# One more feed-forward unit by plain products: block products begin with unit 6 instead of unit 5

## The chip, the cores and the metric

The kernel runs on one core of a Trainium2 chip. The metric is device time in microseconds (us) of one execution; the time of a kernel is the median of its runs. Five engines work side by side: TensorE (PE in the profile; its weight loads are PEld), VectorE (DVE), ScalarE (ACT), GpSimd (POOL) and SyncE (SP, which issues most of the transfers).

## The reference

Two layers of an encoder over 512 tokens of width 1024, in float32. Each layer adds an attention mixer, a cross-attention over 256 memory tokens and a feed-forward part to `x`; a last RMSNorm closes. The change touches the feed-forward part alone:

```python
def conv_ffn(h, w_up, conv_w, conv_b, w_down):
    u = h @ w_up                                  # 512 x 1024 @ 1024 x 5632
    up = jnp.pad(u, ((0, 0), (1, 1), (0, 0)))
    u = up[:, :-2] * conv_w[0] + up[:, 1:-1] * conv_w[1] + up[:, 2:] * conv_w[2] + conv_b
    gate, val = jnp.split(u, 2, axis=-1)          # 2816 columns each
    return (jax.nn.silu(gate) * val) @ w_down
...
x = x + conv_ffn(rms_norm(x, norm_ffn[l]), w_up[l], conv_w[l], conv_b[l], w_down[l])
```

## The kernel before

**Numbers.** TensorE multiplies a rounded format, so each float32 operand is kept as two parts, `hi` (the rounded value) and `lo` (what is left). A plain product is three matmuls (hi by hi, hi by lo, lo by hi) of 128 x 512, which `mm3` writes; all matmuls are recorded on line 101, a helper, so they are told apart by the tiles that they write and read.

**Units.** The 2816 gate and 2816 value columns are cut into 22 units of 128 columns of each. Activations lie with channels on the partitions and the 512 tokens along the free axis. The units run in order; of each unit come a gate and a value array, a width-3 convolution of both (`convolve`: on ACT line 1884 and, on DVE, four instructions of line 1891 for each array, two of them 504 columns wide and two 7), Silu on ACT, a product of both (DVE line 1894) and the split into hi and lo for the down projection (ACT line 1079, DVE line 1080).

**Plain units** (`j < PLAIN`): 8 chunks of 128 channels by three matmuls, for gate and for value: 48 matmuls of 128 x 512. They read the normalised input in `ffn.hi` and `ffn.lo` (tiles `xg`). DVE scales both arrays by the token norm (line 1871) before `convolve`.

**Block units** (`j >= PLAIN`): gate and value of a unit are got by seven half-sized products instead of eight, in the manner of Strassen and Winograd. The tokens are cut into two halves and the channels into two halves; `up_forms` multiplies seven weight forms by seven input forms. A product is 4 chunks of one matmul of 128 x 512 (weight hi by input hi and lo side by side) and one of 128 x 256 (weight lo by input hi), 56 matmuls for a unit. Three banks `a` (tag mm), `b` (tr) and `c` (sc) collect them, and DVE and POOL add pieces between products: three reductions (DVE line 1963) and five additions of 128 x 256 (DVE lines 1971, 1979, 1983, 1984, 1989) for each unit, with ACT copies and POOL additions (lines 1970, 1982) between.

**Forms.** The weight forms `sums` and `diffs` are made ahead in HBM by transfers (`make_form`, an accumulating transfer on POOL's queue), in shares of a few units (`SHARES_OF_FORMS`). The input forms are made once in each layer: `scale_tokens` (DVE line 1913) after unit 0, `token_sums` (DVE and POOL, lines 1924 to 1928) and the splits of `t2` and `t1` after unit 2, and the splits of `t3`, `b22` and `t4` after the last plain unit, because those three are written over `ffn.hi` and `ffn.lo`, which the plain products read until then. In a split, ACT writes hi (lines 1939, 1942) and DVE (POOL for `b22`) writes lo (lines 1940, 1943).

**Weights.** Each weight tile of 512 KB is loaded (SP), rounded to hi by ACT (line 789) and its lo is taken by POOL (line 790), of `sums` by DVE (line 790).

**Down rows.** The units lie in groups (0 to 5, 6 to 11, 12 to 16, 17 to 21). While a group's units run, the rows of the down projection of the group before run between their products (`sequence`); a row of group 0 is 6 plain products of 512 columns, one for each unit. Unit 6 has one row behind it, units 7 to 11 two or less each.

**Order.** The order on PE, ACT, DVE and POOL is set when the program is built: the class `Order` replays the program with costs, moves instructions to where it expects them to be ready, and tries several rounds. So an edit in one place can move instructions anywhere. PE may take later products ahead of ones that are not ready, within the turn of the banks.

Of the kernel before, what the change touches and what calls it, by code (L numbers as in the profile page):

```python
# [35 lines left out]
TURNED = 2  # L36


PLAIN = 5
SHARES_OF_FORMS = [(5, 4), (9, 4), (13, 4), (17, 5)]  # L40
HALF = S // 2
EPS = 1e-6
BIG = 3.0e38
# [640 lines left out]
def encoder_kernel(ctx: ExitStack, tc: tile.TileContext, t: dict, out: bass.AP):  # L684
# [16 lines left out]
    made = [[[dpool.tile([D, P * n], F32, name=f"dr_{what}{l}{j}") for what in ("sums", "diffs")]  # L701
             for j, n in SHARES_OF_FORMS] for l in range(DEPTH)]
    form_queue = [(l, g, n) for l in range(DEPTH) for g in range(len(SHARES_OF_FORMS)) for n in range(4)]

    def make_form(upto=DEPTH):
# [4 lines left out]
        l, g, n = form_queue.pop(0)  # L710
        j, nj = SHARES_OF_FORMS[g]
        w, half = t["w_up"][l], D // 2
# [108 lines left out]
    def plan_up(l, what, j):  # L821
        if what == "up":
            cols(("up", j, 0), t["w_up"][l], 0, KC, P * j, P)
            cols(("up", j, 1), t["w_up"][l], 0, KC, D_FF + P * j, P)
            return
        (g, j0), = [(g, j0) for g, (j0, n) in enumerate(SHARES_OF_FORMS) if j0 <= j < j0 + n]
        if what == "gate":
# [8 lines left out]
    def sequence():  # L836
# [4 lines left out]
        for g, (j0, nj) in enumerate(GROUPS):  # L841
            row = 0
            for j in range(j0, j0 + nj):
                to = 0 if g == 0 else min(KC, 2 * (j - j0) + 1) if j < j0 + nj - 1 else KC
                rows, row = range(row, to), to
                if j < PLAIN:
                    yield "up", j, None
# [350 lines left out]
    for l in range(DEPTH):  # L1198
# [675 lines left out]
        def convolve(j, us):  # L1874
            cs = []
            for side in range(2):
                ch = side * NF + j
                u = us[side]
                if side and j >= PLAIN:
                    w = [minus[:, l, i, j : j + 1] for i in range(3)]  # L1880
# [49 lines left out]
        def split_form(name, where=None):  # L1930


            place = xform[name] = [rtile((2, S)) for _ in range(2)] if where is None else [where[:, :2], where[:, 2:]]
            direct = {"b11": (0, 0), "b21": (1, 0), "b22": (1, 1)}
            for i, v in enumerate(place):
                hi, lo = (v[:, :, half] for half in halves)
                src = quarter(*direct[name])[i] if name in direct else raw_forms[name][:, 2 * i : 2 * i + 2]
                if name in ("t1", "t4"):
                    ACT.mul(hi, src, -1.0)
                    DVE.scalar_tensor_tensor(lo, src, -1.0, f(hi), op0=ALU.mult, op1=ALU.subtract)  # L1940
                else:
                    ACT.copy(hi, src)
                    (POOL if name == "b22" else DVE).tensor_sub(lo, src, f(hi))  # L1943
# [162 lines left out]
        for what, n, rows in sequence():  # L2106
# [15 lines left out]
            elif n > 1:  # L2122
                up(n)
                if n == 2:
                    token_sums()
                    split_form("t2")
                    split_form("t1")
                elif n == PLAIN - 1:
                    split_form("t3", ffn.hi[:, :4])
# [94 lines left out]
```

## Time and profile before

| | before |
|---|---|
| median of 3 runs (lowest to highest) | 1323.54 us (1323.25 to 1324.92) |
| the profiled execution, its own time | 1324.15 us |
| its span in the trace | 1322.3 us |
| mean granted TensorE clock | 0.995 |
| PE, DVE, POOL, ACT busy share of the span | 98%, 70%, 65%, 59% |

The page gives busy times over the whole span. TensorE's share is near one everywhere, but its matmuls are pipelined, so that a recorded one (0.39 us) is longer than the distance to the next one; what TensorE loses is better seen from starts, in a stretch whose number of matmuls is known. The timeline gives starts, the windows give the busy time of each engine and the granted clock in a stretch.

### The profile page before, as it was taken

What the parts mean: (1) busy time and instruction counts of PE and PEld (TensorE: products, weight loads), DVE (VectorE), ACT (ScalarE), POOL (GpSimd) and SP (SyncE); (2) the same over time, 40 slices, a digit from 0 to 9 for tenths busy, and PEclk for the clock granted to TensorE, in tenths of its full rate; (3) what the DMA queues carried; (4) which work ended last, traced back from release to release, by engine and by line L of the source; (5) the groups of instructions that cost most, each with busy time, mean ns of one, the idle gap of its engine ahead of it and who ended that gap; (6) DMA issues with size and microseconds to landing.
All of it is one profiled execution on the core that took longest, in us unless ns stands there. A gap on an engine that the chain in (4) does not pass through costs nothing.

```text
span 1322.3 us, 19671 instructions
## 1 busy us (share of the span) xinstructions
PE 1297.9 (98%) x6715; PEld 1098.2 (83%) x6715; DVE 924.8 (70%) x1883; ACT 781.7 (59%) x1473; POOL 861.2 (65%) x656
## 2 busy tenths in 40 slices
PE   9999999999989999999999999999998999999997
PEld 8888888888878888888888878888887788888887
DVE  6559876675995676666635697775769866666675
ACT  6677776665654554554645687765644545555554
POOL 3657966737666677767745678665566666766673
PEclk9999999999999999999999999999998999999999
DMA  9733698678599788796556427958882455554541
GB/s 285 223 110 102 188 238 195 200 169 221 147 230 241 221 232 219 199 256 171 170 144 191 144 64 210 261 136 257 188 190 77 130 150 151 159 148 141 154 144 64
DMA packets 290564, 235.46 MB, mean 178 GB/s; under 512 B 7712, under 2 KB 246816, under 8 KB 290464
## 3 DMA queue, kind: packets, MB, share of 16 engines
q1 hardware_dynamic: 273152, 198.16, 50.5%
q0 software_dynamic: 16896, 35.65, 15.1%
q8 instruction: 53, 0.87, 0.3%
q14 instruction: 47, 0.39, 0.1%
q10 hardware_dynamic: 416, 0.39, 0.1%
HBM read 224.22 MB, written 73.40 MB: 225 GB/s over the span
## 4 chain that ended last, share of the span: by engine, by line
PE 87%; DVE 9%; ACT 2%; issue 1%; DMA 1%; POOL 0%; POOLq 0%; ACTq 0%; DVEq 0%
PE mm L101 64%; PE sc L101 16%; PE tr L101 4%; PE tr L1586 2%; DVE t L1891 2%; DMA raw<-dr_sums 1%; PE tr L1431 1%; DVE r L1943 1%; DVE lo L790 1%; DVE t L1963 1%; PE tr L1780 1%; DVE r L1080 0%; ACT hi L789 0%; DVE sc L1403 0%; DVE r L1913 0%
## 5 line engine op out<-in xcount | busy, mean ns | idle before, releaser
L790 POOL TENSOR_TENSOR lo<-raw,hi 128x512 fp32r<-128x512 f32 (+3 forms) x327 | 567.3, 1750 | 279.0 <-ACT hi L789 237.0
L789 ACT CAST hi<-raw 128x1024 fp32r<-128x1024 f32 (+2 forms) x365 | 291.2, 813 | 287.5 <-issue 82.4
L101 PE MATMUL mm<-r,hi 128*128 128x512 f32 (+1 forms) x1360 | 442.3, 392 | 6.7 <-DVE t L1963 3.7
L101 PEld LDWEIGHTS mm<-r,hi 128*128 128x128 f32 x1360 | 249.0, 188 | 59.0 <-DVE t L1963 4.0
L101 PE MATMUL mm<-r,lo 128*128 128x512 f32 (+1 forms) x848 | 291.2, 346 | 0.0
L101 PE MATMUL mm<-xg,hi 128*128 128x512 f32 x784 | 258.8, 395 | 4.0 <-DVE sc L1984 2.8
L101 PEld LDWEIGHTS mm<-r,lo 128*128 128x128 f32 x848 | 160.1, 189 | 22.4
L101 PE MATMUL mm<-xg,lo 128*128 128x256 f32 (+1 forms) x528 | 176.6, 334 | 0.0
L101 PEld LDWEIGHTS mm<-xg,hi 128*128 128x128 f32 x784 | 145.8, 188 | 35.2 <-DVE sc L1984 2.3
L101 PE MATMUL mm<-hi,xg 128*128 128x512 f32 (+1 forms) x384 | 111.7, 360 | 0.0
L101 PEld LDWEIGHTS mm<-xg,lo 128*128 128x128 f32 x528 | 99.7, 189 | 11.9
L101 PE MATMUL sc<-xg,hi 128*128 128x512 f32 x328 | 109.0, 395 | 0.0
L1086 POOL TENSOR_SCALAR t<-t,s 128x512 f32<-128x512 f32 (+1 forms) x112 | 67.7, 627 | 43.5 <-DVE s L1570 20.1
L1982 POOL TENSOR_TENSOR t<-t 128x256 f32<-128x256 f32 x34 | 42.4, 1248 | 62.6 <-ACT t L1981 62.6
L1989 DVE TENSOR_TENSOR sc<-mm,t 128x256 f32<-128x256 f32 x34 | 14.7, 432 | 88.4 <-ACT t L1988 88.4
L101 PEld LDWEIGHTS mm<-hi,xg 128*128 128x128 f32 x384 | 68.0, 189 | 9.2 <-DVE r L1280 0.2
L101 PE MATMUL sc<-xg,lo 128*128 128x256 f32 (+1 forms) x232 | 75.4, 327 | 0.0
L101 PE MATMUL sc<-r,r 128*128 128x256 f32 (+1 forms) x352 | 73.2, 329 | 0.0
L101 PEld LDWEIGHTS sc<-xg,hi 128*128 128x128 f32 x328 | 61.4, 188 | 14.0 <-ACT xg L78 0.4
L101 PE MATMUL sc<-r,hi 128*128 128x512 f32 x200 | 72.6, 405 | 0.1
L101 PE MATMUL mm<-lo,xg 128*128 128x512 f32 (+1 forms) x192 | 68.4, 356 | 0.0
L1080 DVE TENSOR_TENSOR r<-tr,r 128x512 fp32r<-128x512 f32 x82 | 55.7, 685 | 14.2 <-ACT r L1079 10.1
(222 smaller groups left out, 2457.2 us busy)
## 6 DMA issues: line engine op xcount, KB each, us to landing
raw<-in_w_up SPq DMA_DIRECT2D x54, 512.0 KB, 4.7
raw<-dr_sums SPq DMA_DIRECT2D x34, 512.0 KB, 4.3
raw<-dr_diffs SPq DMA_DIRECT2D x34, 512.0 KB, 4.3
raw<-in_w_in SPq DMA_DIRECT2D x25, 512.0 KB, 5.0
dr_sums<-in_w_up SPq DMA_DIRECT2D x12, 1024.0 KB, 7.5
dr_diffs<-in_w_up SPq DMA_DIRECT2D x12, 1024.0 KB, 9.1
raw<-in_w_down SPq DMA_DIRECT2D x32, 384.0 KB, 4.0
raw<-in_w_up SPq DMA_DIRECT2D x34, 256.0 KB, 3.1
```

Source lines behind the costliest of these rows:

```text
L101: return self.engine.matmul(out, lhsT, rhs, **k)
L789: act.copy(hi[:, k], raw[:, k])
L790: (POOL if eng[0] == "P" else DVE).tensor_sub(lo[:, k], raw[:, k], f(hi)[:, k])
L1080: DVE.tensor_sub(lo, ps, f(hi))
L1086: eng.tensor_scalar(e, e, sums[:, col : col + 1], 1.0, op0=ALU.mult, op1=ALU.mult)
L1431: PE.transpose(tr[:, (2 * i + c) * P : (2 * i + c + 1) * P], es[j][:, i, c * P : (c + 1) * P], ident)
L1586: PE.transpose(tr[:, k * P : (k + 1) * P], es[j][:, k * P : (k + 1) * P], ident)
L1780: PE.transpose(tr[:, (2 * c + i) * P : (2 * c + i + 1) * P], e[:, i, c * P : (c + 1) * P], ident)
L1891: DVE.scalar_tensor_tensor(cc[:, dst], u[:, src], wi, cc[:, dst], op0=ALU.mult, op1=ALU.add)
L1943: (POOL if name == "b22" else DVE).tensor_sub(lo, src, f(hi))
L1982: POOL.tensor_add(vc, vc, u2)
L1989: DVE.tensor_add(ch, ah, l4)
```

## The change

`PLAIN` goes from 5 to 6: in each layer unit 5 is made by 48 plain matmuls instead of 56 of the block form. The shares of the weight forms move with it: they begin with unit 6, and the last share has four units instead of five. The splits of `t3`, `b22` and `t4` now stand behind unit 5.

```diff
-PLAIN = 5
-SHARES_OF_FORMS = [(5, 4), (9, 4), (13, 4), (17, 5)]
+PLAIN = 6
+SHARES_OF_FORMS = [(6, 4), (10, 4), (14, 4), (18, 4)]
```

The order of instructions shows the change at three places. In the rows, a number behind a name tells buffers apart.

First, DVE in layer 0 from the scaling of the last plain unit's value array on. Before (`sc_3908` is the value array of unit 4; `mm_3970`, `tr_3971`, `sc_3972` are banks a, b, c of unit 5; `r_3783`, `r_3789` are lo parts of t2 and t1, `xg_2894` with `r_3776` is t3, with `r_3779` t4):

```order
L1871 TENSOR_TENSOR sc_3908<-sc_3908,rep_3592 128x512
L790 TENSOR_TENSOR lo_3910<-raw_3725,hi_3909 128x1024
L1963 TENSOR_REDUCE t_3973<-mm_3970 128x256
L1891 SCALAR_TENSOR_TENSOR t_3864<-sc_3825,par,t_3864 128x7
L1943 TENSOR_TENSOR r_3783<-r_3773,r_3783 128x2x256
L1940 SCALAR_TENSOR_TENSOR r_3789<-r_3770,r_3789 128x2x256
L1963 TENSOR_REDUCE t_3974<-mm_3970 128x256
L1943 TENSOR_TENSOR xg_2894<-r_3776,xg_2894 128x2x256
L1963 TENSOR_REDUCE t_3975<-sc_3972 128x256
L1971 TENSOR_TENSOR tr_3971<-tr_3971,t_3973 128x256
L1940 SCALAR_TENSOR_TENSOR xg_2894<-r_3779,xg_2894 128x2x256
L1979 TENSOR_TENSOR t_3975<-mm_3970,t_3975 128x256
```

Now (`sc_3989` is the value array of unit 5; `mm_4053` and `sc_4055` are banks a and c of unit 6; `mm_3794`, `mm_3877`, `mm_3958` are the gate arrays of the plain units 3, 4 and 5):

```order
L1871 TENSOR_TENSOR sc_3989<-sc_3989,rep_3592 128x512
L1891 SCALAR_TENSOR_TENSOR t_3858<-mm_3794,par,t_3858 128x7
L1943 TENSOR_TENSOR xg_2894<-r_3776,xg_2894 128x2x256
L1963 TENSOR_REDUCE t_4056<-mm_4053 128x256
L1891 SCALAR_TENSOR_TENSOR t_3858<-mm_3794,par,t_3858 128x504
L1891 SCALAR_TENSOR_TENSOR t_3858<-mm_3794,par,t_3858 128x7
L1891 SCALAR_TENSOR_TENSOR t_3941<-mm_3877,par,t_3941 128x504
L1891 SCALAR_TENSOR_TENSOR t_3941<-mm_3877,par,t_3941 128x7
L1891 SCALAR_TENSOR_TENSOR t_4022<-mm_3958,par,t_4022 128x504
L1963 TENSOR_REDUCE t_4057<-mm_4053 128x256
L1894 TENSOR_TENSOR mm_3794<-mm_3794,t_3864 128x512
L1963 TENSOR_REDUCE t_4058<-sc_4055 128x256
```

The weight split of `sums` and the lo parts of t2 and t1 no longer stand behind the end of the plain part; the convolutions of units 3, 4 and 5 do.

Second, TensorE at the end of the first block unit's `diffs` products in layer 0. Before (`hi_3976` is the `diffs` weight of unit 5, `hi_4002` the gate weight of unit 6):

```order
L101 MATMUL sc_3972<-xg_2895,hi_3976 128x512
L101 MATMUL sc_3972<-xg_2895,lo_3977 128x256
L101 MATMUL tr_4056<-r_3681,lo_4003 128x256
L101 MATMUL tr_4056<-r_3681,hi_4002 128x512
L101 MATMUL tr_4056<-r_3681,lo_4003 128x256
L101 MATMUL tr_4056<-r_3682,hi_4002 128x512
```

Now (`hi_4059` is the `diffs` weight of unit 6, `hi_4085` that of down row 0, `mm_4136` its bank; `r_3610`, `r_3660`, `r_3767`, `r_3872`, `r_3955` are the activations of units 0 to 4; `tr_4163` is bank b of unit 7):

```order
L101 MATMUL sc_4055<-xg_2895,hi_4059 128x512
L101 MATMUL sc_4055<-xg_2895,lo_4060 128x256
L101 MATMUL mm_4136<-r_3610,hi_4085 128x512 x2
L101 MATMUL mm_4136<-r_3610,lo_4086 128x512
L101 MATMUL mm_4136<-r_3660,hi_4085 128x512 x2
L101 MATMUL mm_4136<-r_3660,lo_4086 128x512
L101 MATMUL mm_4136<-r_3767,hi_4085 128x512 x2
L101 MATMUL mm_4136<-r_3767,lo_4086 128x512
L101 MATMUL mm_4136<-r_3872,hi_4085 128x512 x2
L101 MATMUL mm_4136<-r_3872,lo_4086 128x512
L101 MATMUL mm_4136<-r_3955,hi_4085 128x512
L101 MATMUL tr_4163<-r_3681,lo_4110 128x256
```

A down row now stands between the `diffs` products of the first block unit and the gate products of the next.

Third, DVE in layer 1 from the scaling of the last plain unit's gate array on. Before (`mm_10441` and `sc_10472` are gate and value of unit 4, `lo_10474` is the lo part of the `sums` weight of unit 5, `mm_10534` its bank a):

```order
L1871 TENSOR_TENSOR mm_10441<-mm_10441,rep_10160 128x512
L1943 TENSOR_TENSOR r_10250<-r_10234,r_10250 128x2x256
L790 TENSOR_TENSOR lo_10474<-raw_10291,hi_10473 128x1024
L1891 SCALAR_TENSOR_TENSOR t_10430<-sc_10391,par,t_10430 128x504
L1943 TENSOR_TENSOR r_10349<-r_10339,r_10349 128x2x256
L1891 SCALAR_TENSOR_TENSOR t_10430<-sc_10391,par,t_10430 128x7
L1940 SCALAR_TENSOR_TENSOR r_10354<-r_10336,r_10354 128x2x256
L1871 TENSOR_TENSOR sc_10472<-sc_10472,rep_10160 128x512
L1891 SCALAR_TENSOR_TENSOR t_10430<-sc_10391,par,t_10430 128x504
L1963 TENSOR_REDUCE t_10537<-mm_10534 128x256
```

Now (`mm_10486` and `sc_10517` are gate and value of unit 5, `mm_10579` is bank a of unit 6):

```order
L1871 TENSOR_TENSOR mm_10486<-mm_10486,rep_10124 128x512
L1891 SCALAR_TENSOR_TENSOR t_10475<-sc_10436,par,t_10475 128x504
L1891 SCALAR_TENSOR_TENSOR t_10388<-mm_10324,par,t_10388 128x504
L1891 SCALAR_TENSOR_TENSOR t_10475<-sc_10436,par,t_10475 128x7
L1940 SCALAR_TENSOR_TENSOR r_10319<-r_10300,r_10319 128x2x256
L1891 SCALAR_TENSOR_TENSOR t_10388<-mm_10324,par,t_10388 128x7
L1943 TENSOR_TENSOR xg_9426<-r_10306,xg_9426 128x2x256
L1871 TENSOR_TENSOR sc_10517<-sc_10517,rep_10124 128x512
L1891 SCALAR_TENSOR_TENSOR t_10388<-mm_10324,par,t_10388 128x504
L1963 TENSOR_REDUCE t_10582<-mm_10579 128x256
```

Between the last two scalings stood the weight split of `sums` and three lo parts; now two lo parts stand there, and the weight split has gone ahead.

## The prediction

> **What bounds the kernel now.** I read the page first, then the waits of TensorE, then its timeline around the edit, then the windows.
>
> ```profile
> span 1322.3 us, 19671 instructions
> PE 1297.9 (98%) x6715; PEld 1098.2 (83%) x6715; DVE 924.8 (70%) x1883; ACT 781.7 (59%) x1473; POOL 861.2 (65%) x656
> PE 87%; DVE 9%; ACT 2%; issue 1%; DMA 1%; POOL 0%; POOLq 0%; ACTq 0%; DVEq 0%
> ```
>
> The third row is the chain that ended last: TensorE carries 87% of it and DVE 9%. So matmuls cost their full time, and other work counts only where TensorE waits for it. Who it waits for (total us, times, longest):
>
> ```profile
> PE mm L101 <- DVE t L1963: 3.7, 1, 3.7
> PE mm L101 <- DVE sc L1984: 2.8, 2, 1.9
> PE sc L101 <- DVE lo L790: 1.8, 2, 1.1
> PE mm L101 <- DVE xg L1943: 1.1, 1, 1.1
> ```
>
> Three of these four (1963, 1984, 1943) are DVE's work for block units and for input forms. Where they lie, TensorE's timeline shows (start, us, what; in brackets the idle time before). A steady stretch first:
>
> ```profile
> 348.47 0.62 PE L101 MATMUL mm<-xg,hi 128*128 128x512 f32 x2
> 359.35 0.39 PE L101 MATMUL mm<-r,hi 128*128 128x512 f32 x1
> ...
> 425.92 0.40 PE L101 MATMUL mm<-xg,hi 128*128 128x512 f32 x1
> 430.16 0.64 PE L101 MATMUL mm<-r,hi 128*128 128x512 f32 x2
> 434.31 0.39 PE L101 MATMUL mm<-xg,hi 128*128 128x512 f32 x1
> ```
>
> From 348.47 to 359.35 runs plain unit 4 of layer 0: 10.88 us. From 425.92 to 430.16 stand 12 pairs (512 and 256 columns) of block products: 0.353 us each. From 430.16 to 434.31 runs one down row, 6 triples: 4.15 us. A block unit has 28 pairs, so 9.89 us.
>
> Now the stretch from unit 5's first product to the start of down row 1, in layer 0 (from 359.35 above to the first row here) and layer 1 (the other rows):
>
> ```profile
> 393.91 0.62 PE L101 MATMUL mm<-r,hi 128*128 128x512 f32 x2
> ...
> 1009.84 0.39 PE L101 MATMUL mm<-r,hi 128*128 128x512 f32 x1
> 1016.76 0.80 PE L101 MATMUL mm<-r,hi 128*128 128x512 f32 x1 [3.71 <-DVE t L1963]
> 1032.26 0.50 PE L101 MATMUL mm<-xg,hi 128*128 128x512 f32 x1 [1.93 <-DVE sc L1984]
> 1050.71 0.63 PE L101 MATMUL mm<-r,hi 128*128 128x512 f32 x2
> ```
>
> By the order it holds units 5 and 6 whole (56 pairs), gate and sums of unit 7 (16 pairs) and down row 0: 72 x 0.353 + 4.15 = 29.6 us. It took 34.56 us in layer 0 and 40.87 in layer 1. TensorE loses 5.0 and 11.3 there, together **16.3 us**. Why, the windows tell (length, then busy us of PE, PEld, DVE, ACT, POOL, then the granted clock):
>
> ```profile
> 348.00:359.00 11.00, 11.00 (x50) 9.11 (x49) 11.00 (x15) 8.48 (x13) 6.65 (x6) 1.00 0.35 83
> 359.00:370.00 11.00, 9.39 (x50) 7.47 (x49) 10.59 (x13) 4.26 (x7) 10.32 (x6) 1.00 0.76 134
> 1012.60:1015.70 3.10, 0.45 (x3) 0.12 (x1) 3.10 (x3) 0.19 (x1) 1.71 (x1) 1.00 0.91 256
> 1015.70:1022.60 6.90, 5.84 (x18) 4.97 (x19) 4.65 (x7) 1.36 (x3) 4.10 (x3) 0.51 0.29 82
> 1022.60:1032.80 10.20, 7.39 (x42) 6.03 (x41) 9.30 (x19) 3.78 (x6) 5.29 (x4) 1.00 0.36 103
> 1032.80:1036.30 3.50, 3.50 (x13) 2.92 (x12) 2.50 (x7) 1.99 (x4) 0.96 (x2) 0.51 0.57 164
> ```
>
> DVE is full before and across the boundary: it brings a queue of work into the first block unit. In layer 1 the clock adds to it: half of 6.9 us and of 3.5 us at 0.51, some 5 us of the 11.3.
>
> **The change part by part.** *Unit 5 on TensorE.* 10.88 instead of 9.89 us, on the path: +0.99 us a layer, **+1.98**.
>
> *Unit 5 on DVE.* The steps, start to start:
>
> ```profile
> 375.82 0.73 DVE L1891 SCALAR_TENSOR_TENSOR t<-sc,par,t 128x504 f32<-128x504 f32 x1
> 376.47 0.21 DVE L1891 SCALAR_TENSOR_TENSOR t<-mm,par,t 128x7 f32<-128x7 f32 x1
> 376.61 0.21 DVE L1891 SCALAR_TENSOR_TENSOR t<-sc,par,t 128x7 f32<-128x7 f32 x1
> ...
> 387.70 0.41 DVE L1979 TENSOR_TENSOR t<-mm,t 128x256 f32<-128x256 f32 x1
> 388.03 0.42 DVE L1983 TENSOR_TENSOR tr<-sc,t 128x256 f32<-128x256 f32 x1
> ...
> 388.83 1.22 DVE L790 TENSOR_TENSOR lo<-raw,hi 128x1024 fp32r<-128x1024 f32 x1
> 389.96 0.68 DVE L1963 TENSOR_REDUCE t<-mm 128x256 f32<-128x512 f32 x1
> 390.56 0.68 DVE L1999 TENSOR_TENSOR xT<-xT,mm 128x512 f32<-128x512 f32 x1
> ```
>
> So 0.65 for 504 columns, 0.14 for 7, 0.33 for 256, 0.60 for a whole bank, 1.13 for a weight split. A convolution with product and split is 4 x 0.65 + 4 x 0.14 + 2 x 0.60 = 4.36. A plain unit adds two scalings: 5.56 us of DVE under 10.88 of TensorE. A block unit adds three reductions, five additions and the split of sums: 1.80 + 1.65 + 1.13, so 8.94 under 9.89. DVE's spare time in unit 5 grows from 0.95 to 5.32 us, and by the order the first block unit, now unit 6, has a down row (4.15 us for 0.60 of DVE) ahead of its closing product. That is how the 16.3 us can go.
>
> *What is left in layer 0.* The last wait that decides is line 1984, which frees bank a for the closing `val` product. In the order after, DVE has from the last plain scaling up to it 12 steps of 0.60, 7 of 0.65, 8 of 0.14 and 4 of 0.33: 14.2 us, begun 0.2 after TensorE's last plain product (row below). TensorE comes to that product after 32 pairs and the row: 11.3 + 4.15 = 15.45. Before, it came there after the 32 pairs alone, 11.3, and DVE was ready at 373.45 + 0.43, 14.5 after 359.35. The spare is 1.0 us where nothing collides. But instructions with two operands in SBUF stretch when POOL works:
>
> ```profile
> 359.56 0.70 DVE L1871 TENSOR_TENSOR sc<-sc,rep 128x512 f32<-128x512 f32 x1 [0.41 <-PE sc L101]
> 365.91 2.26 DVE L1943 TENSOR_TENSOR xg<-r,xg 128x512 fp32r<-128x512 f32 x1
> 373.45 0.43 DVE L1984 TENSOR_TENSOR sc<-mm,t 128x256 f32<-128x256 f32 x1
> ```
>
> The middle row is the lo part of t3, 2.26 where the same width elsewhere takes 0.68. One such collision is 1.66; between none and two the wait left is 0 to 2.3. I take one and a third (t3 again, t4 in part): 2.2 - 1.0 = **1.2 us**.
>
> *What is left in layer 1.* Here DVE was late before the first block product:
>
> ```profile
> 1006.95 3.42 DVE L790 TENSOR_TENSOR lo<-raw,hi 128x1024 fp32r<-128x1024 f32 x1
> ...
> 1012.15 2.72 DVE L1940 SCALAR_TENSOR_TENSOR r<-r,r 128x512 fp32r<-128x512 f32 x1
> 1014.78 0.69 DVE L1871 TENSOR_TENSOR sc<-sc,rep 128x512 f32<-128x512 f32 x1
> ...
> 1016.03 0.67 DVE L1963 TENSOR_REDUCE t<-mm 128x256 f32<-128x512 f32 x1
> ...
> L1943 DVE TENSOR_TENSOR r<-r,r 128x512 fp32r<-128x512 f32 x12 | 14.0, 1166 | 0.0
> ```
>
> The scaling of the last plain value array came at 1014.78, 4.9 after TensorE had ended that unit, behind a split stretched to 3.42 and a lo part stretched to 2.72; the reduction behind it let TensorE go on at 1016.76. In the order after, DVE has from unit 4's last scaling to unit 5's, while TensorE works 10.88 us: two scalings, three steps of 0.65, three of 0.14, the split and five lo parts. With no collision that is 7.7; with every one as long as the longest rows here (3.42, three of 2.26, two of 2.72) 19.2. With the group's mean of 1.17 for a lo part (1.09 from start to start) and 2.3 for the split, half way between 1.13 and 3.42, it is 11.3: 0.4 late. I take this value, since the mean comes from these very instructions. With layer 0's 1.2 that is 1.6 us. The bounds are 0 and 8.3 + 2.3 = 10.6.
>
> *The clock.* After the idle 3.71 us the clock stood at 0.51 for 6.9 us, after the idle 1.93 at 0.51 for 3.5; in layer 0, with waits up to 1.1, it stayed at 1.00 (row 359 to 370). So a single wait near 2 us may cost another 1.7, and I add 0.7 for it: **2.3 us** in layer 1. [...]
>
> *Transfers, POOL and ACT.* Unit 5 loads two weight tiles of 512 KB instead of three and a half, and POOL splits two of them instead of two and a half, without the two small additions; the shares of forms begin a unit later and the last is a fifth smaller. SP's queue issues fewer transfers and DMA was 0.76 busy in that stretch, so I cost this at nothing; it is hidden under 10.88 us of TensorE, and if the cover failed, the new tile late would be unit 5's value weight. The splits of t3, b22 and t4 wait for unit 5's plain products, as before for unit 4's; behind them on ACT stand Silu and the casts of unit 3, on POOL the weight splits of down row 0 and unit 7. Down row 0 needs unit 5's activation in its last triple; DVE has it 13.1 us after the plain end (the 14.2 without its last three steps), TensorE comes there after 30 pairs and five triples, at 14.0.
>
> *Elsewhere.* The planner orders the rest anew. The waits outside the two stretches, like the 1.8 us for line 790, can grow or shrink; I take 0, and 2 us either way for the range.
>
> *Sum.* 1324.15 (the profiled execution) - 16.3 + 1.98 + 1.2 + 2.3 = 1313.3. That execution lies 0.6 above the median of 1323.54, so the forecast is **1312.7 us**, 0.8% faster.
>
> **Rivals.** *A, layer 1 keeps half:* the lo parts there collide again, DVE is 4 us late at the last scaling and the half clock comes back once at its full 3.4. For it: the stretched rows 3.42 and 2.72 come from POOL's splits, and those still stand there. Against: another 10.88 us of plain products now lie between them and the block unit. Layer 1 then keeps 7.5: 1324.15 - 16.3 + 1.98 + 1.2 + 7.5 - 0.6 = 1317.9.
>
> *B, the gain is eaten:* layer 1 keeps all its 11.3 and layer 0 2.0, as at the upper bound of the split and lo parts. 1324.15 - 16.3 + 1.98 + 13.3 - 0.6 = 1322.5, no difference that shows.
>
> *C, slower:* the waits belong to the boundary, not to unit 5. t3, b22 and t4 can't be written until the last plain product has read its operands, wherever that stands, and a block unit needs t3 within its first 5.6 us. If all 16.3 come back at unit 6, the plain unit's 1.98 is left: 1325.5. It decides from the point where more than 14.3 us of waits remain. For it: the wait for line 1943 (1.1) is of that kind. Against: it is the only one; the reduction and line 1984 are late from DVE's queue.
>
> *D, all goes:* no collision, no wait left: 1324.15 - 16.3 + 1.98 - 0.6 = 1309.2.
>
> **Numbers.** The forecast with its smaller variations has 0.58 (own range 1310 to 1316), A 0.18, D 0.09, B 0.08, C 0.07. 0.2% is 2.6 us, about what a measurement of this kernel can tell from no change. Faster by more: forecast, A and D, 0.85. Within: most of B and some of C, 0.08. Slower: the rest, 0.07. The range leaves out B and C and reaches from D with 1 us of luck elsewhere (1308.2) to A with 1.6 us of loss (1319.5): 0.85 less its edges, 0.8.
>
> **What would show it.** The stretch from unit 5's first product to down row 1 should take 30.6 us (29.6 + 0.99) plus what is left: 31 to 33 in layer 0, 31 to 34 in layer 1, against 34.6 and 40.9. DVE should reach the last plain scaling in layer 1 within 1 us of TensorE's end; the wait for line 1963 should be under 1 us, that for line 1984 under 2 in all; the granted clock should stay at 1.00 there, or fall once for 3.5 us. TensorE should have 16 matmuls fewer. The forecast is wrong if POOL's splits meet DVE's lo parts later but as long, so that line 1963 or 1943 still holds TensorE for 3 us, or if the new order opens waits over 2 us in attention.

## Result and profile after

The changed kernel takes 1304.52 us (median of 4 runs, 1304.26 to 1304.64) against 1324.23 us for the kernel before in the same comparison (4 runs): a ratio of 0.9851, 95% interval 0.9834 to 0.9868. It is 19.7 us faster; 10.8 were forecast, and the time lies 3.7 us below the range.

The page of the changed kernel, its span, its busy times and the shares of the chain that ended last:

```profile
span 1302.5 us, 19581 instructions
PE 1292.3 (99%) x6699; PEld 1096.4 (84%) x6699; DVE 916.0 (70%) x1869; ACT 776.6 (60%) x1463; POOL 857.7 (66%) x650
PE 95%; DVE 3%; ACT 1%; issue 1%; POOL 0%; POOLq 0%; DVEq 0%; ACTq 0%
```

DVE's share of the chain fell from 9% to 3%. TensorE's waits over the whole span (total us, times, longest) are now these:

```profile
PE tr L101 <- POOL ident masks.py:199: 1.4, 1, 1.4
PE tr L1431 <- DVE r L1297: 0.8, 1, 0.8
PE mm L101 <- DVE t L1963: 0.6, 1, 0.6
PE mm L101 <- DVE t L1457: 0.4, 2, 0.2
PE tr L101 <- DVE r L1080: 0.3, 1, 0.3
```

The waits for lines 1984, 1943 and 790 are gone, and the one for 1963 lies at 460 us, outside the two stretches. Where the 19.8 us of span went is read from two marks in DVE's timeline, the first scaling of a layer's feed-forward part (line 1871) and the addition of down row 1 (the second of line 1999). Before, for both layers:

```profile
322.06 1.30 DVE L1871 TENSOR_TENSOR mm<-mm,rep 128x512 f32<-128x512 f32 x2 [7.64 <-ACT rep L1002]
398.21 0.69 DVE L1999 TENSOR_TENSOR xT<-xT,mm 128x512 f32<-128x512 f32 x1
972.55 0.70 DVE L1871 TENSOR_TENSOR mm<-mm,rep 128x512 f32<-128x512 f32 x1 [7.64 <-ACT rep L1002]
1055.05 0.68 DVE L1999 TENSOR_TENSOR xT<-xT,mm 128x512 f32<-128x512 f32 x1
```

After:

```profile
322.07 1.30 DVE L1871 TENSOR_TENSOR mm<-mm,rep 128x512 f32<-128x512 f32 x2 [7.79 <-ACT rep L1002]
394.65 0.68 DVE L1999 TENSOR_TENSOR xT<-xT,mm 128x512 f32<-128x512 f32 x1
963.77 1.30 DVE L1871 TENSOR_TENSOR mm<-mm,rep 128x512 f32<-128x512 f32 x2 [7.64 <-ACT rep L1002]
1036.55 0.68 DVE L1999 TENSOR_TENSOR xT<-xT,mm 128x512 f32<-128x512 f32 x1
```

| piece | before | after | difference | forecast |
|---|---|---|---|---|
| start to layer 0's first scaling | 322.06 | 322.07 | 0.0 | 0 |
| layer 0, first scaling to down row 1 | 76.15 | 72.58 | -3.6 | -5.0 + 0.99 + 1.2 = -2.8 |
| from there to layer 1's first scaling | 574.34 | 569.12 | -5.2 | 0 |
| layer 1, first scaling to down row 1 | 82.50 | 72.78 | -9.7 | -11.3 + 0.99 + 2.3 = -8.0 |
| from there to the end of the span | 267.25 | 265.95 | -1.3 | 0 |

By these marks the two stretches gave 13.3 us where 10.8 were expected, and 6.5 us came from where nothing was expected. The marks are DVE's, though, and in the changed kernel TensorE does 1.1 us more of its later work ahead of them. With the work counted on TensorE itself the pieces become sharper. The forecast puts 110 matmuls of 512 columns and 44 of 256 into a stretch from unit 5's first product to down row 1. In after, TensorE starts 112 and 44 from 359.21 to 390.14 and from 1001.07 to 1032.06; less 2 x 0.23 us for the two too many, that is 30.5 us in each layer, against 34.56 and 40.87 before. So the stretches gave 4.1 and 10.3, together **14.4 us, and 5.4 us came from elsewhere** (5.3 in the expectations below, which go by the times of the runs).

### The profile page after: what moved, and what is told of

Read it like the earlier page. It is cut to its first block, busy times and chain, and to the rows that moved or that the text cites. A ratio compares the mean times of both kernels' runs of the same rounds, so it can differ in the third digit from the quotient of the medians.

```text
span 1302.5 us, 19581 instructions
## 1 busy us (share of the span) xinstructions
PE 1292.3 (99%) x6699; PEld 1096.4 (84%) x6699; DVE 916.0 (70%) x1869; ACT 776.6 (60%) x1463; POOL 857.7 (66%) x650
## 4 chain that ended last, share of the span: by engine, by line
PE 95%; DVE 3%; ACT 1%; issue 1%; POOL 0%; POOLq 0%; DVEq 0%; ACTq 0%
PE mm L101 69%; PE sc L101 18%; PE tr L101 4%; PE tr L1586 2%; PE tr L1431 1%; PE tr L1780 1%; DVE t L1891 0%; DVE r L1080 0%; DVE sc L1403 0%; PE tr L1501 0%; DVE r L1129 0%; DVE t L1456 0%; DVE t L1489 0%; ACT r L1079 0%; ACT t L1409 0%
## 5 line engine op out<-in xcount | busy, mean ns | idle before, releaser
L789 ACT CAST hi<-raw 128x1024 fp32r<-128x1024 f32 (+3 forms) x361 | 287.8, 814 | 274.4 <-issue 71.3
L101 PE MATMUL mm<-r,hi 128*128 128x512 f32 (+1 forms) x1344 | 432.8, 390 | 0.0
L101 PE MATMUL mm<-r,lo 128*128 128x512 f32 (+1 forms) x832 | 286.5, 347 | 0.0
L101 PE MATMUL mm<-xg,lo 128*128 128x512 f32 (+1 forms) x528 | 177.9, 337 | 0.0
L101 PEld LDWEIGHTS mm<-r,lo 128*128 128x128 f32 x832 | 156.4, 188 | 22.6 <-POOL lo L790 0.5
L101 PE MATMUL sc<-xg,hi 128*128 128x512 f32 x352 | 116.3, 395 | 0.0
L101 PE MATMUL sc<-xg,lo 128*128 128x256 f32 (+1 forms) x240 | 79.4, 332 | 0.0
L101 PEld LDWEIGHTS sc<-xg,hi 128*128 128x128 f32 x352 | 66.1, 189 | 14.5 <-ACT xg L78 0.4
L101 PE MATMUL sc<-r,hi 128*128 128x512 f32 x192 | 68.7, 398 | 0.0
L790 DVE TENSOR_TENSOR lo<-raw,hi 128x1024 fp32r<-128x1024 f32 (+1 forms) x36 | 44.2, 1229 | 33.8 <-ACT hi L789 33.5
```

Of the source, the lines that this page charges most:

```text
L101: return self.engine.matmul(out, lhsT, rhs, **k)
L789: act.copy(hi[:, k], raw[:, k])
L790: (POOL if eng[0] == "P" else DVE).tensor_sub(lo[:, k], raw[:, k], f(hi)[:, k])
```

## The experiments

Each was timed beside the kernel before on the same chip; the ratio is to that. One table serves them all: us in which TensorE stood still, by stage. A gap counts where the distance between the starts of two neighbouring matmuls exceeds its usual value (0.23 us for 512 columns, 0.12 for 256) by more than 0.2 us. "Boundary" runs from a layer's first scaling to the addition of down row 1, "rest 0" from there to the end of layer 0, "attention 1" to layer 1's first scaling. In the rows, a kernel called after or before "in another order" does the same work with another planned order.

| kernel | time, us | boundary 0 | rest 0 | attention 1 | boundary 1 |
|---|---|---|---|---|---|
| before (profile at 1324.15) | 1324.23 | 4.5 | 1.6 | 3.3 | 7.6 |
| after | 1304.52 | 0 | 0.8 | 0.3 | 0 |
| e1, layer 0 alone | 1313.14 | 0 | 0.8 | 0.4 | 8.2 |
| e2, layer 1 alone | 1314.68 | 5.8 | 1.1 | 2.9 | 0.4 |
| e3, the row without the plain unit | 1328.54 | 7.9 | 0.9 | 2.1 | 9.2 |
| e4, the plain unit without the row | 1306.05 | 1.2 | 0 | 0.4 | 1.0 |
| e5, e6, e13, e14: before in other orders | 1322.07, 1325.00, 1323.14, 1322.47 | 5.8, 7.5, 6.0, 7.6 | 1.8, 1.6, 2.1, 2.2 | 3.0, 2.5, 2.6, 2.2 | 5.3, 4.8, 6.7, 5.1 |
| e7, e8, e15, e16: after in other orders | 1305.38, 1304.91, 1305.60, 1305.06 | 0 in all | 0.3, 0.3, 0.8, 0.8 | 0.8, 0.5, 0.3, 0 | 0 in all |
| e9, unit 5's splits on DVE | 1306.09 | 0 | 0.8 | 0 | 0 |
| e10, before with unit 5's sums split on POOL | 1319.91 | 4.0 | 0.9 | 2.8 | 5.9 |
| e11, seven plain units | 1298.62 + 8.3 | 0 | 0.8 | 0 | 0 |
| e12, before with the shares moved | 1324.30 | 4.5 | 2.2 | 3.3 | 7.4 |

**One layer at a time (e1, e2).** `PLAIN` and the shares become lists by layer:

```diff
-PLAIN = 5
+PLAINS = (6, 5)      # e1; e2: (5, 6)
```

> The edit in layer 0 alone (unit 5 plain there, block form in layer 1). Theory 1 (each layer's waits come from DVE's queue at that layer's own boundary, and the rest of the gain is the new order elsewhere): the stretch from unit 5's first product to down row 1 takes 30.5 to 31 us in layer 0 and stays at 40 to 41 in layer 1 with the half clock; 1324.2 - 4.2 = 1320.0 us, 1.5 either way for the order elsewhere. Rival (the 5 us gained outside the two stretches belong to layer 0's edit): 1315 us or less, with the waits of 0.8 to 1.3 us in layer 1's attention gone.

> The edit in layer 1 alone. Theory 1: layer 0's stretch stays at 34 to 35 us, layer 1's falls to 30.5 to 31 and its half clock goes: 1324.2 - 10.3 = 1313.9 us, 1.5 either way. Rival (what is gained outside belongs to layer 1's edit): 1309 us or less.

e1 took 1313.14 us, ratio 0.9924 (0.9909 to 0.9939), e2 1314.68, 0.9937 (0.9923 to 0.9952). The kernel before took 1322.99 beside them, so the gains are 9.9 and 8.3 us, 18.2 together; the time of after lies 18.5 below that, so the layers add up. e2 came where the theory expected it. e1 did not: layer 0's edit is worth 9.9 us where the theory gave it 4.2, and the rival's range, 1315 or less, holds. TensorE's waits of e1 from 1000 to 1040 us and of e2 from 359 to 395, each in the layer without the edit (lines are one higher here):

```profile
PE mm L102 <- DVE lo L791: 4.1, 2, 2.1
PE mm L102 <- DVE t L1964: 2.8, 3, 1.3
...
PE mm L102 <- DVE t L1964: 3.0, 1, 3.0
PE mm L102 <- DVE sc L1990: 1.1, 1, 1.1
PE mm L102 <- DVE t L1892: 0.9, 1, 0.9
```

The boundary waits stay in the layer that still has five plain units, and go in the other. But e1 also lost attention's waits in layer 1, which it does not touch, and layer 1's half clock: its waits of 8.2 us there passed at full clock (1.00 from 1003 to 1045 us). The piece between the marks of the two layers, 574.3 us before, took 569.3 in e1 and 572.9 in e2.

**The row or the plain unit (e3, e4).** The edit does two things at the boundary: it gives DVE slack in unit 5, and it puts a down row into the first block unit. e3 has the second alone, e4 the first alone:

```diff
-GROUPS = [(0, 6), (6, 6), (12, 5), (17, 5)]
+GROUPS = [(0, 5), (5, 6), (11, 6), (17, 5)]      # e3, with PLAIN = 5
+GROUPS = [(0, 7), (7, 5), (12, 5), (17, 5)]      # e4, with PLAIN = 6
```

> Unit 5 in block form as before, but the groups of the down projection are cut as 0 to 4, 5 to 10, 11 to 16, 17 to 21, so that the first block unit has a down row behind it. Theory 1 (DVE's spare time in a plain unit 5 is what dissolves the queue): DVE still comes to the first block unit with its queue, so the waits for the first reduction and for t3 stay (1 us in layer 0, 3 to 4 and the half clock in layer 1) and only the wait for line 1984 goes, about 3 us of the two layers: 1318 to 1322 us. Rival (the down row ahead of the first closing product is the cover): both stretches lose their waits and no plain unit is paid: 1324.2 - 16.3 + 1 = 1309 us or less.

> Unit 5 plain as in the changed kernel, but the groups are cut as 0 to 6, 7 to 11, 12 to 16, 17 to 21, so that the first block unit (6) has no down row behind it. Theory 1: most waits stay away, since DVE's queue is shorter by 4 to 5 us at the boundary; the wait for line 1984 comes back with about 2 us a layer, because its cover of 4.15 us is gone and 1 us of it was spare: 1304.5 + 4 = 1306 to 1310 us. Rival (the down row is the cover): 5 us or more of waits in each layer come back, with the half clock in layer 1: 1314 us or more.

e3 took 1328.54 us, ratio 1.0035 (1.0022 to 1.0048); e4 1306.05, 0.9871 (0.9856 to 0.9885). Waits of e3 from 1010 to 1045 us, and then of e4 from 355 to 400:

```profile
PE mm L101 <- DVE t L1963: 5.2, 2, 2.7
PE sc L101 <- DVE lo L790: 2.3, 1, 2.3
...
PE mm L101 <- DVE sc L1984: 0.2, 1, 0.2
```

The row alone does not help; it came out 5.5 us slower than before, where the theory had 1318 to 1322: the first block unit comes behind five units' convolutions as before, and the half clock returns four times (0.50 or 0.51 for 3.4 us each), two of them in layer 0. The plain unit alone brings 16.9 us beside its before of 1322.99, and its time lies 1.5 us above after's. The row covers what is left, 1.2 us of waits in layer 0 and 1.0 in layer 1, mostly for the activations. That the plain unit works by giving DVE slack is seen where DVE comes to the gate scaling of unit 5 in after: in both layers it stood idle and waited for TensorE, so it had caught up. Before, the last gate scaling, that of unit 4, came without such a wait.

```profile
364.85 0.70 DVE L1871 TENSOR_TENSOR mm<-mm,rep 128x512 f32<-128x512 f32 x1 [0.45 <-PE mm L101]
1006.71 0.70 DVE L1871 TENSOR_TENSOR mm<-mm,rep 128x512 f32<-128x512 f32 x1 [0.45 <-PE mm L101]
```

One part of e4's expectation failed. The wait for line 1984 should have come back with about 2 us a layer without its cover; it came with 0.2 us in layer 0 and not at all in layer 1. The planner had set convolutions behind line 1984 instead of ahead of it: in e4's layer 0 the last plain scaling starts at 370.21, and this row ends 11.1 us later, where after takes 14.9:

```profile
380.88 0.43 DVE L1984 TENSOR_TENSOR sc<-mm,t 128x256 f32<-128x256 f32 x1
```

So what DVE has to do ahead of line 1984 is no fixed load; it hangs on the order that the planner finds.

**Is it the order's luck (e5 to e8, e13 to e16)?** The planner tries its orders with a seed, and keeps corrections for windows of 500 instructions. Both kernels were built with two other seeds and two other window sizes; the work is the same:

```diff
-ROUNDS, REPLAYS, MARGIN, SHARES, STRETCH, SEED = 12, 4, 100.0, (0.0, 0.0, 0.5, 1.0, 2.0), 500, 4
+... 500, 5   and   ... 500, 6   and   ... 480, 4   and   ... 600, 4
```

> The kernel before with another seed of the planner; the work is the same, and only the order in which its replays break ties and move instructions differs. Theory 1 (the waits at the boundary come from VectorE's full queue there, 5.0 us in layer 0 and 11.3 in layer 1; the 5.3 us that the change gained outside the two stretches is an accident of the order): the stretch from unit 5 to down row 1 keeps 4 us or more of waits in each layer, while the small waits elsewhere come and go; time 1318 to 1329 us. Rival (the order of before was an unlucky draw, boundary and all): 1312 us or less.

> As the other seed. Theory 1: 1318 to 1329 us, waits of 4 us or more in each of the two stretches. Rival: 1312 us or less.

> The changed kernel with another seed of the planner. Theory 1 (the two stretches are clean because VectorE has slack in a plain unit 5; the 5.3 us elsewhere is an accident of the order): the stretches keep under 2 us of waits each, and some of the 5.3 us elsewhere is given back; time 1305 to 1311 us. Rival 2 (the 5.3 us elsewhere follows from the change itself, since VectorE and GpSimd have less to do): 1303 to 1306 us. Rival 3 (the clean stretches were themselves a lucky draw): 1312 us or more, with waits of 3 us or more in a stretch.

> As the other seed of the changed kernel. Theory 1: 1305 to 1311 us. Rival 2: 1303 to 1306 us. Rival 3: 1312 us or more.

> The kernel before, the planner's windows cut at 480 instructions instead of 500; the work is the same. Theory 1 (the three waits of layer 1's attention come from how the windows fall): they shrink from 3.0 us in all to under 1, and 1318 to 1322 us is measured with the stretches at the boundary as they were. Rival (they follow from five plain units in layer 0, by the state in which the attention starts): 2 us or more stay, 1321 to 1327 us.

> As with 480, now with windows of 600. Theory 1: under 1 us of waits in layer 1's attention in at least one of the two kernels. Rival: 2 us or more in both, 1321 to 1327 us.

> The changed kernel with windows of 480 instructions. Theory 1 (windows): layer 1's attention gets waits of 1 us or more in at least one of the two variants of the changed kernel, 1304 to 1308 us. Rival: under 1 us in both, 1303.5 to 1306 us.

> As with 480, now with windows of 600. Theory 1: 1 us or more of waits in layer 1's attention here or with 480. Rival: under 1 us in both, 1303.5 to 1306 us.

The ratios are 0.9984 (0.9975 to 0.9993), 1.001 (1.0 to 1.0019), 0.9994 (0.9984 to 1.0003) and 0.9997 (0.9988 to 1.0007) for before, and 0.9857 (0.9842 to 0.9872), 0.9857 (0.9842 to 0.9871), 0.9865 (0.985 to 0.988) and 0.9861 (0.9846 to 0.9876) for after. Five orders of before lie within 3 us, five of after within 1.1, and all five of after have no wait in the stretches, though DVE was only just in time there. My theory, that the gain outside the stretches was an accident of the order, falls, and with it the one on windows: it follows from the change. TensorE's waits from 700 to 960 us (layer 1's attention) of before, then of e13, then of after:

```profile
PE mm L101 <- DVE t L1457: 1.1, 1, 1.1
PE tr L1431 <- POOL t L1496: 0.7, 1, 0.7
PE tr L1501 <- DVE r L1080: 0.6, 1, 0.6
...
PE mm L101 <- ACT hi L789: 1.0, 1, 1.0
PE tr L1501 <- DVE r L1080: 0.6, 1, 0.6
PE tr L1431 <- POOL t L1496: 0.3, 1, 0.3
...
PE mm L101 <- DVE t L1457: 0.2, 1, 0.2
```

The table says the same of all: 2.1 us or more in each kernel whose layer 0 has five plain units, 0.8 or less where it has six or seven.

**The shares alone (e12).**

```diff
-SHARES_OF_FORMS = [(5, 4), (9, 4), (13, 4), (17, 5)]
+SHARES_OF_FORMS = [(5, 5), (10, 4), (14, 4), (18, 4)]
```

> The kernel before with the shares of the weight forms alone moved: (5, 5), (10, 4), (14, 4), (18, 4), so that the last share has four units, as in the changed kernel, and the products stay as before. Open is what took the three waits of layer 1's attention (0.8, 0.9 and 1.3 us) away. Theory 1 (the plain unit of layer 0, by way of the planned order; the shares cost and bring nothing): the three waits stay, 1322 to 1326 us. Rival (the smaller transfers on GpSimd's queue): the three waits go, 1319 to 1321.5 us.

1324.30 us, ratio 1.0004 (0.9994 to 1.0013), and attention keeps 3.3 us: the smaller transfers are not what took its waits.

**The price of work on DVE (e9, e10).** In the changed kernel line 1984 ends only just ahead of TensorE, so more work on DVE should show at once; and less work on DVE should help the kernel before.

```diff
-            cols(("up", j, 0), t["w_up"][l], 0, KC, P * j, P)            # e9; (up, j, 1) in the same way
+            cols(("up", j, 0), t["w_up"][l], 0, KC, P * j, P, "D" if j == 5 else "P")
-            cols(("sums", j), made[l][g][0], 0, KC, P * (j - j0), P, "D")     # e10, in the kernel before
+            cols(("sums", j), made[l][g][0], 0, KC, P * (j - j0), P, "P" if j == PLAIN else "D")
```

> The changed kernel with the lo parts of unit 5's two weights taken by VectorE instead of GpSimd, in both layers: 2 x 1.13 us more in VectorE's queue under unit 5 (3.0 with the 1.50 that such a split takes there beside GpSimd), and some 7 us less on GpSimd. Theory 1 (VectorE's queue sets the waits; in the changed kernel line 1984 is done only 0.44 us before TensorE needs it in layer 0 and 0.09 us in layer 1): 2 to 3 us of waits come back in each layer, time 1307 to 1312 us. Rival (the waits come from GpSimd's splits, which stretch VectorE's instructions with two operands in SBUF; with fewer of them nothing is lost): 1303 to 1306 us.

> The kernel before with the lo part of the sums weight of unit 5 taken by GpSimd instead of VectorE, in both layers: 1.13 us (layer 0, unstretched) to 3.42 us (layer 1, as it ran) less in VectorE's queue at the boundary, one more split on GpSimd, and no other change of the work. Theory 1 (each us taken out of VectorE's queue is one us of wait less, and no half clock after it): 1316 to 1321 us, with 1 us gained in layer 0 and 3 to 6 in layer 1. Rival (the 16 us hang on that one split alone, since it stands at the queue's narrowest place): 1312 us or less. Rival 2 (GpSimd is then late with the lo part itself, and TensorE waits for that instead): 1322 us or more.

e9 took 1306.09 us, ratio 0.9867 (0.9852 to 0.9881): just outside the rival's range and below the theory's, with no wait at either boundary. A likely reason is in the groups of instructions. Of after, then of e9 (count, busy us, mean ns):

```profile
L790 DVE TENSOR_TENSOR lo<-raw,hi 128x1024 fp32r<-128x1024 f32 (+1 forms) x36 | 44.2, 1229 | 33.8 <-ACT hi L789 33.5
L1926 DVE TENSOR_TENSOR r<-r,r 128x512 f32<-128x512 f32 x4 | 8.7, 2166 | 0.0
L1940 DVE SCALAR_TENSOR_TENSOR r<-r,r 128x512 fp32r<-128x512 f32 x4 | 5.1, 1272 | 0.0
...
L790 DVE TENSOR_TENSOR lo<-raw,hi 128x1024 fp32r<-128x1024 f32 (+1 forms) x40 | 49.5, 1239 | 33.4 <-ACT hi L789 33.4
L1926 DVE TENSOR_TENSOR r<-r,r 128x512 f32<-128x512 f32 x4 | 2.7, 682 | 0.0
L1940 DVE SCALAR_TENSOR_TENSOR r<-r,r 128x512 fp32r<-128x512 f32 x4 | 2.7, 681 | 0.0
```

Four more splits cost DVE 5.3 us, but with four fewer on POOL the token sums and the lo parts of t1 ran unstretched and cost 8.4 us less; DVE's busy time in all fell from 916.0 to 912.8 us. Read so, a split moved to DVE is paid back by the collisions that it no longer causes. So e9 did not test what it was meant to, a longer DVE queue; the size of DVE's slack in the changed kernel is not known better from it. Of the 1.6 us that it is slower than after, 1.1 lie ahead of layer 0's first scaling, where the edit changes nothing; the rest are small steps.

e10 took 1319.91 us, ratio 0.9972 (0.9962 to 0.9981), in the theory's range: a shorter queue, a smaller wait. In its profile (span 1316.7 us) layer 1's boundary stretch takes 78.2 us instead of 82.5, as expected; its waits fell from 7.6 to 5.9 us and the half clock did not come (1.00 from 1003 to 1045 us). Layer 0's stretch changed by 0.2 only, where 1 us was expected.

**A seventh plain unit (e11).**

```diff
-PLAIN = 6
-SHARES_OF_FORMS = [(6, 4), (10, 4), (14, 4), (18, 4)]
+PLAIN = 7
+SHARES_OF_FORMS = [(7, 4), (11, 4), (15, 4), (19, 3)]
```

> Plain products for units 0 to 6 in both layers, shares of forms (7, 4), (11, 4), (15, 4), (19, 3). Theory 1 (the changed kernel has no wait left at the boundary, so a further plain unit only costs its 0.99 us a layer on TensorE): 1304.5 + 2.0 = 1306.5, 1305.5 to 1308 us. Rival (VectorE, with still more slack, goes on removing waits outside the boundary, of which some 3 us are left in the feed-forward parts and layer 1's attention): 1303 to 1305 us.

The code runs down rows only behind block units, so this kernel leaves out down row 0 of each layer's first group, 18 matmuls a layer: 6647 matmuls against 6699 after, 52 fewer, of which 16 by the plain units and 36 by the rows. It took 1298.62 us, ratio 0.9809 (0.9794 to 0.9824). With 2 x 4.15 us added for the rows that is 1306.9, an estimate, against 1306.5 expected: where no wait is left to remove, a plain unit costs about its 0.99 us a layer. By this estimate seven units are 2.4 us slower than six; no kernel with all its rows was timed.

## Why the prediction was wrong

*The bound and the cause: right.* DVE's queue at the end of the plain part held TensorE, and the stretches lost what was read, 5.0 and 11.3 us: they gave 4.1 and 10.3 after paying 0.99 each for the plain unit. e1, e2 and e4 show that a plain unit 5 dissolves it, e3 that the row does not, and rival C (the waits belong to the boundary wherever it stands) is out.

*Unit 5 on TensorE, +1.98: right.* In after it runs from 359.21 to 370.09, 10.88 us:

```profile
359.21 0.62 PE L101 MATMUL mm<-xg,hi 128*128 128x512 f32 x2
370.09 0.39 PE L101 MATMUL mm<-r,hi 128*128 128x512 f32 x1
385.70 0.39 PE L101 MATMUL mm<-xg,hi 128*128 128x512 f32 x1
1011.95 0.39 PE L101 MATMUL mm<-r,hi 128*128 128x512 f32 x1
1027.54 0.46 PE L101 MATMUL mm<-xg,hi 128*128 128x512 f32 x1
```

*What is left, 1.2 us in layer 0: mis-sized, it was 0.* TensorE's arrival at the closing product was right, 385.70 - 370.09 = 15.6 (15.45 forecast). DVE's time was the term that failed. The rows that decide in layer 0, then in layer 1:

```profile
366.89 1.87 DVE L1940 SCALAR_TENSOR_TENSOR r<-r,r 128x512 fp32r<-128x512 f32 x1
368.68 1.77 DVE L1943 TENSOR_TENSOR xg<-r,xg 128x512 fp32r<-128x512 f32 x1
370.38 0.69 DVE L1871 TENSOR_TENSOR sc<-sc,rep 128x512 f32<-128x512 f32 x1
371.12 1.05 DVE L1943 TENSOR_TENSOR xg<-r,xg 128x512 fp32r<-128x512 f32 x1
384.84 0.42 DVE L1984 TENSOR_TENSOR sc<-mm,t 128x256 f32<-128x256 f32 x1
...
1012.25 0.69 DVE L1871 TENSOR_TENSOR sc<-sc,rep 128x512 f32<-128x512 f32 x1
1014.29 1.54 DVE L1943 TENSOR_TENSOR xg<-r,xg 128x512 fp32r<-128x512 f32 x1
1027.03 0.42 DVE L1984 TENSOR_TENSOR sc<-mm,t 128x256 f32<-128x256 f32 x1
```

From the last scaling to the end of line 1984 DVE took 385.26 - 370.38 = 14.9 us, not 14.2 + 2.2: instead of one and a third collisions (2.2 us) the collision there cost 0.4 (1.05 for 0.68). The longer ones, 1.87 and 1.77, fell ahead of the last scaling, into the slack under unit 5, where they held nobody. I had priced collisions at what they cost in the kernel before, though the change moved the steps to a place with room for them. TensorE was 0.44 us behind DVE in layer 0 and 0.09 in layer 1 (1027.54 against 1027.45). In layer 1 it took 15.2, with a collision of 0.9 (1.54 for 0.68). Nor were the 14.2 us a given: in e4, without the row, the planner left 11.1 us there.

*Layer 1, 1.6 + 0.7 us: mis-sized, it was 0.* The last scaling began 0.3 us after TensorE's last plain product (1012.25 against 1011.95; 0.4 forecast, partly by luck: the split of `sums` took 1.5 us there, not 2.3, and DVE stood idle 0.45 in between). That lateness was absorbed: the row ahead of the closing product covers it together with the steps behind it, and layer 0's 1.2 us, counted again here, was not there. The 0.7 us for the half clock was not called for, as no wait came. This window of after from the first block product on shows TensorE busy throughout at full clock (length, then busy us of PE, PEld, DVE, ACT, POOL, then the granted clock):

```profile
1012.20:1023.00 10.80, 10.80 (x61) 9.34 (x60) 10.69 (x22) 6.96 (x12) 8.17 (x6) 1.00 0.49 137
```

What the half clock went with in these traces is worked out in the last section.

*Elsewhere, 0 with 2 us either way: wrong, it was -5.4 us.* This is the larger part of the miss of 8.9 us; the two terms above, 1.2 and 2.3 us, are the rest. I took the rest of the program as re-ordered without a tendency. Ten orders show one: 2.2 to 3.3 us of waits in layer 1's attention in all five of before, 0 to 0.8 in all five of after, and 1.6 to 2.2 against 0.3 to 0.8 in the rest of layer 0. Of the 5.4 us, 3.0 are attention's waits, 0.8 each the rest of layer 0 and of layer 1 (there 1.24 us of waits became 0.41); the other 0.8 are in no gap that the table counts. e1 and e2 tie attention's part to layer 0's edit, e12 rules the shares out, e13 to e16 the planner's windows. Which link carries it over 350 us is not settled: the work there is the same, but the planner set its order anew too.

*Rivals.* For the stretches D came true (nothing left); with its own 1309.2 us it still missed the other 4.7, since it too took 0 elsewhere. The forecast's direction and cause held, its range did not: it allowed for one us of luck on the good side.

## What to carry to other kernels

When one engine's queue makes another wait at a transition, count the slack that a change gives the late engine over the whole piece ahead of it; the stretched instructions that landed in slack (1.87 and 1.77 us in layer 0 of after) cost nothing here, so they are not to be priced at what they cost where there was none. Work moved from GpSimd to VectorE cost less than its own duration in e9: four more splits took 5.3 us of VectorE, and its token sums and lo parts of t1, which then ran unstretched, 8.4 us less. And before an unexplained gain elsewhere is called luck of the order, build both kernels in several orders: here the spread was 1 to 3 us and the gain stood clear of it.

## What the hardware showed

*In these traces the half clock came after an interval of 3.41 us in which TensorE had been idle for 1.93 us or more, once for 1.7; the length of a single wait did not tell it.* In one trace (e14) TensorE waited 2.16 us in layer 0 and 1.94 in layer 1. Behind the waits stand intervals of 3.41 us, two that hold the first wait, the one that holds the second, and the next (length, then busy us of PE, PEld, DVE, ACT, POOL, then the granted clock):

```profile
364.35 0.50 PE L101 MATMUL mm<-r,hi 128*128 128x512 f32 x1 [2.16 <-DVE t L1963]
1017.09 0.50 PE L101 MATMUL mm<-r,hi 128*128 128x512 f32 x1 [1.94 <-DVE t L1963]
...
359.73:363.14 3.41, 2.46 (x14) 1.85 (x13) 3.41 (x5) 2.76 (x5) 3.24 (x3) 1.00 0.87 247
363.14:366.55 3.41, 2.20 (x12) 1.93 (x13) 3.41 (x6) 0.00 (x0) 3.41 (x4) 1.00 0.70 202
1015.09:1018.50 3.41, 1.47 (x9) 1.22 (x9) 3.41 (x4) 1.79 (x4) 3.41 (x4) 1.00 0.85 238
1018.50:1021.91 3.41, 3.41 (x13) 2.92 (x12) 3.08 (x6) 0.00 (x0) 1.45 (x1) 0.50 0.28 81
```

The longer wait left the clock at 1.00, the shorter was followed by 0.50 for 3.4 us. The edges of the intervals are counted from where the clock changes. In before it changes at 1015.75, 1022.58, 1032.82 and 1036.23 us, 296, 298, 301 and 302 times 3.413 us from its first record, and the four spells of e3 start 20.5, 638.3 and 17.1 us apart, 6, 187 and 5 times that; in e5, e6 and e13 too the two spells start a whole multiple of it apart. Counted back from the spell of e14, an edge cuts the first wait, so that the intervals hold 0.95 and 1.21 us of idle time; the second lies whole in one, with 1.94.

Read in steps of 0.5 us from 355 to 395 and from 1003 to 1045 us, the traces of before, e2, e3, e5, e6, e13 and e14 show 14 spells at half clock. Each of the 13 intervals at full clock with 1.93 us of idle time or more was followed by one at half. The fourteenth spell came after one with about 1.7 (e6); others with 1.76 (e14) and 1.87 (e3) had no spell behind them. Two spells lasted 6.8 us instead of 3.4, the first of before and the second of e6; TensorE was idle for 1.0 us within their first 3.41 us, for 0.5 or less in the other twelve. e1 passed waits of 1.96 and 2.10 us at 1.00; it has no spell from which edges could be counted. So a single wait near 2 us was or was not followed by the half clock, and in e14, by this count, the difference was where it fell. In the spell of e14 a pair of 512 and 256 columns took 0.64 us from start to start, against 0.35 at full clock: by that a spell of 3.41 us cost 1.5 us, an estimate, where 1.7 was forecast. The changed kernel stays clear of it: counted from its first clock record, from 7 to 1293 us no interval holds over 0.7 us of idle time.

*VectorE and GpSimd.* The group of line 1926, two operands in SBUF, took 2166 ns in after and 682 in e9: 1.5 us more for each instruction with the same operands. In layer 1 of after the two ran at 991.78 (2.50 us) and 997.90 (1.83 us), beside weight splits of GpSimd that began at 991.34 and 996.78 and took 2.4 us each; in e9 GpSimd has one split in that place, from 997.90, which only the end of the second (997.56, 0.68 us) met. Line 1963, which reads a bank, took 0.68 to 0.69 us in after throughout, though GpSimd worked beside most of its 96 instructions. Nor did every row with both operands in SBUF stretch: in before the lo part at 999.83 (line 1943) took 0.68 us with GpSimd's line 1924 beside it from 999.98.
